# A half-swap of an 8192 x 8192 matrix by DMA: one issuing queue in place of two

## The chip, the cores and the metric

The kernel runs on one core of a Trainium2 chip. Its time is the time of one execution on the device, in microseconds (us), given as the median of several runs. One further execution was recorded by the hardware profiler; all durations inside the kernel come from that one.

The core has compute engines (TensorE, VectorE, ScalarE, GpSimd) that this kernel does not use, and 16 DMA engines, which copy bytes between memories. A DMA is asked for by an instruction on one of the sequencers, here SP (the sync queue, `nc.sync`) or ACT (the scalar queue, `nc.scalar`). The asking is called an issue; the copying is done later by the DMA engines, packet by packet. Input and output both lie in the chip's large memory, HBM.

## The reference

```
def setup_inputs():
    return {"x": np.random.randn(8192, 8192).astype(np.float32)}

def reference(x):
    return np.fft.ifftshift(x)
```

With even sizes, `ifftshift` moves the element at row r, column c to row (r + 4096) mod 8192, column (c + 4096) mod 8192. The four quarters of the matrix change places crosswise; nothing is computed. 8192 x 8192 x 4 bytes = 268.44 MB are read and as many are written.

## The kernel before

The whole kernel is a list of copies from HBM to HBM. There is no on-chip buffer and no compute instruction.

A row has `C` = 8192 elements, 32 KB; half a row, `hc` = 4096 elements, is 16 KB and lies in one piece. The loop at line 27 walks over the output in groups of 512 rows (`ENGINES * per` = 16 x 32), so it has 16 rounds. In a round, `src_row` (line 28) is the first row of the source group, 4096 rows further on, modulo 8192. The inner loop at line 29 makes two DMAs:

- on `nc.sync` with `h` = 0: it writes the left halves of the 512 output rows and reads the right halves of the 512 source rows (column offset `hc - h` = 4096);
- on `nc.scalar` with `h` = `hc`: it writes the right halves and reads the left halves.

Both use the access pattern `dims` of line 26, read from the outside in: 16 rows that follow one another (step `C`), for each of them 32 rows that are 16 rows apart (step `16 * C`), and for each of these 4096 elements in one piece. The outermost dimension has the size 16, as many as there are DMA engines; an engine's share is 32 half rows, row e, e + 16, e + 32 and so on. One DMA moves 512 x 16 KB = 8.39 MB, and there are 32 of them, 16 on each queue.

Nothing in the program depends on anything else, since every output element is written once and the input is never written. The order on each queue is the order of the loop. The framework gives the DMAs eight completion semaphores in turn; a DMA that is to use one again waits until the one that used it before has landed. With the two queues taking turns, that is the DMA four places earlier on the same queue. At the end SP waits for all that is still under way.

Of the kernel before, what the change touches and what calls it, by code (L numbers as in the profile page):

```python
# [1 line left out]

# [4 lines left out]


ENGINES = 16


@with_exitstack
def kernel(
    ctx: ExitStack,
    tc: tile.TileContext,
    x: bass.AP,
    out: bass.AP,
):
    nc = tc.nc
    R, C = x.shape  # L20
    hr = R // 2
    hc = C // 2


    per = 32
    dims = [[C, ENGINES], [ENGINES * C, per], [1, hc]]
    for row in range(0, R, ENGINES * per):
        src_row = (row + hr) % R
        for queue, h in ((nc.sync, 0), (nc.scalar, hc)):
            queue.dma_start(  # L30
                out=bass.AP(out.tensor, out.offset + row * C + h, dims),
                in_=bass.AP(x.tensor, x.offset + src_row * C + hc - h, dims),
            )


# [1 line left out]
_INS = ['x']  # L37
_OUTS = [((8192, 8192), 'float32')]


def kernel(**inputs):
    import numpy as _np
    import concourse.bacc as _bacc
    import concourse.tile as _tile
    from concourse import mybir as _mybir
    from concourse.bass_utils import run_bass_kernel_spmd as _run

    nc = _bacc.Bacc("TRN2", target_bir_lowering=False, num_devices=1)  # L48
    arrays, args = {}, []
    for name in _INS:  # L50
        a = _np.ascontiguousarray(inputs[name])
        if a.dtype.kind in "iu":
            a = a.astype(_np.int64)
        arrays[f"in_{name}_dram"] = a
        args.append(nc.dram_tensor(f"in_{name}_dram", a.shape, _mybir.dt.from_np(a.dtype), kind="ExternalInput").ap())
    for i, (shape, dtype) in enumerate(_OUTS):
        dt = _mybir.dt.from_np(_np.dtype(dtype))
        args.append(nc.dram_tensor(f"out_{i}_dram", shape, dt, kind="ExternalOutput").ap())
    with _tile.TileContext(nc) as tc:
        kernel(tc, *args)  # L60
    r = _run(nc, [arrays], core_ids=[0])
    got = tuple(r.results[0][f"out_{i}_dram"] for i in range(len(_OUTS)))
    return got[0]
```

## Time and profile before

| | us |
|---|---|
| median of 3 runs | 823.65 |
| lowest and highest | 820.24, 824.01 |
| the profiled execution | 822.98 |
| its span, from first to last instruction | 821.2 |

The profiled execution is the one that the page and all queries show. "Span" runs from its first to its last instruction.

In the page's second part the span is cut into 40 equal slices: the row `DMA` gives, in tenths, how busy the 16 DMA engines were on average, the row `GB/s` how much they moved (counted once, not for read and write separately). The third part has one row for each DMA queue: packets, megabytes, and the time that its packets took as a share of 16 engines over the whole span. A query can be given a window of the span, and then answers for that window alone. For DMA issues the profile also gives the duration of the issuing instruction and the time from its start until the data had landed:

| line 30 | issues | shortest issue, us | median issue, us | longest issue, us |
|---|---|---|---|---|
| on SP | 16 | 0.571 | 41.264 | 47.309 |
| on ACT | 16 | 0.579 | 42.036 | 48.448 |

From issue to landing the median is 204.0 us on SP and 204.1 us on ACT; over all issues the shortest is 51.6 and the longest 207.1 us. SP's issues begin at 0.7 us and the last begins at 614.2 us; ACT's last begins at 618.8 us. After that both sequencers only wait for transfers to finish.

### The profile page before, as it was taken

To read this page: it belongs to the slowest core of one execution; us is meant where nothing else is said; L and a number is where in the kernel's file an instruction comes from. 1 tells how busy PE (TensorE), PEld (TensorE's weight loads), DVE (VectorE), ACT (ScalarE), POOL (GpSimd) and SP (SyncE) were. 2 spreads that over 40 slices of the span, in tenths; PEclk is the share of its full clock that TensorE was granted. 3 is DMA by queue.
4 is the path that set the end of the run, shared out by engine and by line. 5 is a ranking of instruction groups with operands and counts; after the bars stand their busy time and mean duration, and the time that the engine had idled before them with its cause. 6 is when DMAs were issued, how large, how long until landed. Compare 5 with 4: busy or idle time off the path is not lost. (4 is left out here: it accounts for less than half of the span.)

```text
span 821.2 us, 77 instructions
## 1 busy us (share of the span) xinstructions
POOL 0.2 (0%) x4
## 2 busy tenths in 40 slices
POOL 0000000000000000000000000000000000000000
DMA  8999999999999999999999999999999999999998
GB/s 296 333 324 329 331 328 334 330 330 329 327 330 329 331 326 332 332 327 328 330 330 330 330 323 330 324 330 330 332 326 329 330 322 333 329 329 327 330 329 276
DMA packets 16896, 268.44 MB, mean 327 GB/s; under 512 B 512, under 2 KB 512, under 8 KB 512
## 3 DMA queue, kind: packets, MB, share of 16 engines
q1 hardware_dynamic: 8448, 134.22, 50.2%
q10 hardware_dynamic: 8448, 134.22, 49.0%
HBM read 268.44 MB, written 268.44 MB: 654 GB/s over the span
## 5 line engine op out<-in xcount | busy, mean ns | idle before, releaser
L48 POOL MEMSET const-bfloat16-1.0<- 128x1 bf16 x1 | 0.1, 102 | 0.0
L48 POOL MEMSET const-uint8-127<- 128x1 uint8 x1 | 0.1, 102 | 0.0
L48 POOL MEMSET const-float32-0.0<- 128x1 f32 x1 | 0.1, 99 | 0.2 <-issue 0.2
L48 POOL MEMSET const-float32-1.0<- 128x1 f32 x1 | 0.1, 99 | 0.0
## 6 DMA issues: line engine op xcount, KB each, us to landing
out_dram<-in_x_dram ACTq DMA_DIRECT2D x16, 8192.0 KB, 204.1
out_dram<-in_x_dram SPq DMA_DIRECT2D x16, 8192.0 KB, 204.0
```

Source lines behind the costliest of these rows:

```text
L48: nc = _bacc.Bacc("TRN2", target_bir_lowering=False, num_devices=1)
```

## The change

The inner loop no longer chooses a queue. Both DMAs of a round are issued on `nc.sync`, first the one that writes the left halves of the 512 rows, then the one that writes the right halves of the same rows.

```
--- before
+++ after
     for row in range(0, R, ENGINES * per):
         src_row = (row + hr) % R
-        for queue, h in ((nc.sync, 0), (nc.scalar, hc)):
-            queue.dma_start(
+        for h in (0, hc):
+            nc.sync.dma_start(
                 out=bass.AP(out.tensor, out.offset + row * C + h, dims),
                 in_=bass.AP(x.tensor, x.offset + src_row * C + hc - h, dims),
             )
```

The 32 DMAs, their sizes, their access patterns and their order in the program are the same. SP has 32 issues instead of 16, and ACT has none. The eight completion semaphores are still given in turn, so a DMA now waits for the one eight places earlier on the same queue.

## The prediction

> **What bounds the kernel now.** I read the page first. No compute engine does anything (POOL is busy for 0.2 us); the chain of waits is empty beyond the first half microsecond. What is left is the DMA part:
>
> ```profile
> span 821.2 us, 77 instructions
> ...
> DMA  8999999999999999999999999999999999999998
> GB/s 296 333 324 329 331 328 334 330 330 329 327 330 329 331 326 332 332 327 328 330 330 330 330 323 330 324 330 330 332 326 329 330 322 333 329 329 327 330 329 276
> DMA packets 16896, 268.44 MB, mean 327 GB/s; under 512 B 512, under 2 KB 512, under 8 KB 512
> ...
> q1 hardware_dynamic: 8448, 134.22, 50.2%
> q10 hardware_dynamic: 8448, 134.22, 49.0%
> HBM read 268.44 MB, written 268.44 MB: 654 GB/s over the span
> ```
>
> The two queues together keep 16 engines busy for 99.2% of the span, 0.992 x 821.2 = 814.6 us. Each engine moves 1024 of the 16,384 data packets (268.44 MB / 16,384 = 16 KB, half a row), so a packet takes 814.6 / 1024 = 0.795 us. (The 512 small packets, 16 for each of 32 DMAs, announce completions.) The other 0.8%, 6.6 us, is the head and the tail. So the time is 1024 x T + 6.6 us, T being the mean packet time, and the change must act on T or open gaps between packets.
>
> Is T = 0.795 us what an engine needs? The trace has two stretches in which one queue is alone. In the first microseconds only q1 has packets: the second table below is the window from 3.7 to 5.1 us. At the end q1 has finished its data and q10 is alone: the window from 815.4 to 817.5 us. (q1 is SP's: in the first 60 us SP's DMAs land after a median of 152.9 us, ACT's after 156.8, and q1 is ahead.)
>
> ```profile
> DMA packets 36, 0.59 MB, mean 421 GB/s; under 512 B 0, under 2 KB 0, under 8 KB 0
> ...
> q1 hardware_dynamic: 36, 0.59, 101.9%
> ```
>
> ```profile
> DMA packets 56, 0.67 MB, mean 320 GB/s; under 512 B 15, under 2 KB 15, under 8 KB 15
> ...
> q10 hardware_dynamic: 45, 0.66, 88.3%
> q1 hardware_dynamic: 11, 0.02, 4.0%
> ```
>
> In the first, 16 full engines move 421 GB/s, a packet in 16 x 16,384 B / 421 GB/s = 0.623 us. In the second, 0.66 MB take 0.883 x 16 x 2.1 = 29.7 engine-us: 22.2 GB/s per engine, 356 GB/s for 16, 0.736 us per packet. (Some engines have run dry, which is why the plain rate is 320.) The body, by the same sum, is at 16 x 16,384 / 0.795 = 330. So with one queue alone packets were quicker, at both ends. That is the strongest thing the trace says about this change, and it is thin: 1.4 and 2.1 us. Windows of 2.1 us in the middle, where both queues run, scatter as widely:
>
> ```profile
> 400.00:402.10 2.10, 0.00 (x0) 1.00 0.91 296
> 402.10:404.20 2.10, 0.00 (x0) 1.00 1.07 351
> ...
> 412.60:414.70 2.10, 0.00 (x0) 1.00 0.98 320
> 414.70:416.80 2.10, 0.00 (x0) 1.00 1.01 359
> ```
>
> (Columns: window, its length, POOL's busy time, clock, DMA share, GB/s.) The end stretch is at the top of that scatter; the start stretch is above it.
>
> **The change part by part.**
>
> 1. *ACT's 16 DMA issues go, SP gets 16 more.* Issuing is no path here if the queue never runs dry. The row of line 30 gives SP's issues 0.571 us at least and 41.3 us in the median: the long ones stand blocked until the queue has room. SP's fourth issue ended 46.4 us after the first began, when most of the first DMA's data had moved; so one queue takes in about three DMAs, 3 x 8.39 MB = 25 MB, 76 us of work at 330 GB/s. 32 issues at 0.571 us are 18 us in 821, all under transfers. Cost nothing; the cover is those 76 us, and it is lost only if SP is late by more than that. Behind a blocked issue on SP stand only the next issues and the final waits; nobody else waits for SP. ACT's queue is then empty, which costs nothing.
>
> 2. *The waits.* SP waited 123.8 us in 11 waits on earlier DMAs in the first 600 us, each for the DMA four places back on its own queue (51.3 us the longest), always with other DMAs queued. In one stream these waits fall on older DMAs. Bounds: no gain (the engines were full) and no loss (the same 76 us of cover). I take 0.
>
> 3. *The start.* The first packet moves 2.2 us into the span and is SP's; it stays. ACT's packets came in after 5.1 us (the window up to there holds none), when SP's had all engines busy (DMA share about 1.0 from 2.2 us on): 0. The end: 3.7 us after 817.5, the last engines and the landing. One queue ends with the same uneven engines: 0, at most -2 to +2 us.
>
> 4. *What lies side by side changes: the whole case.* Before, each engine alternates between the queues: a right half read to the left, then, from a row some steps behind, a left half to the right. In the first 20 us q1 has 208 packets and q10 154, so ACT trails by 54 / 16 = 3.4 packets per engine, and as engine e's rows are 16 apart, by some 54 rows or 1.8 MB. After, all 16 engines work in one such place at a time, and for 25 us the reads are all right halves and the writes all left ones. No row has this for long. Upper bound of the gain: T = 0.623, 1024 x 0.623 + 6.6 = 645 us. Next row: T = 0.736, 754 + 6.6 = 760 us. No gain: 821. Loss: see the last rival. The two quick stretches are short, and the longer is the less quick. I take half of what the end stretch shows, since it lies within the scatter of ordinary windows: T = (0.736 + 0.795) / 2 = 0.766, 784 + 7 = 791 us.
>
> A rule speaks against this. The Trainium skill, "DMA: Bandwidth & Descriptors", section "Issuing engines are not separate DMA queues", says that DMAs from different issuing engines interleave on the same 16 engines, so that several issuers save issue time and no more. The one-queue stretches at 421 and 356 GB/s beside 330 don't bear that out, weakly; by the rule the sum is 821 again. The same page, "Latency and other measured facts", reports copies whose rows lie 2 MiB apart at 164 GB/s where 512 KiB apart gave 207, and guesses at aliasing in HBM; ACT's trail of 1.8 MB is near that. Should that ratio (0.79) be the whole loss of the body, an estimate from that page is 0.79 x 815 + 7 = 651 us of span; no run here shows it.
>
> **Sum.** 791 us of span for the forecast. Around the profiled execution's 821.2 us lie 1.8 us (its time is 822.98), and the median of the runs shown is 823.65, 0.7 above it. 791 + 1.8 = 793 us, 3.7% under the median.
>
> **The rivals.**
>
> *No change, 823 us.* The engines and HBM carry the same bytes in packets of the same size; 654 GB/s of reads and writes is the limit of the path, and 421 at the start is what buffers take in before it fills. For it: 38 of the 40 slices lie at 322 to 334 GB/s whatever rows are moved. Against it: the windows by microsecond fall only as q10 comes in (377 and 455 GB/s up to 5.1 us, 393, 328 and 377 after it), and the end stretch is quick long after any start. A chance of 0.19.
>
> *The start rate lasts, 647 us.* If the two streams hinder each other in HBM and one doesn't, T stays near 0.623: 645 + 1.8. For it: 36 packets at that rate, from all 16 engines. Against it: the end stretch is not that quick, and reads and writes still meet. With what lies between it and the forecast's own range (under 750 us) 0.12.
>
> *Slower: one queue stumbles at the end of each DMA, 842 us.* Every DMA ends on every engine with a completion packet, after which the next DMA's packets begin. Before, the other queue's packets stand ready at that moment; after, nothing else does. Price: what the engines lost as they began. The first microsecond of packets moved 246 GB/s against 421 soon after, (421 - 246) / 421 = 0.42 us lost. At 31 boundaries 13 us; at 0.8 us, were the next one late as well, 25: 836 to 848, middle 842. If each DMA drained as the kernel's end does, 3.7 us, it would be 115 us more: 938. It decides from 4 / 31 = 0.13 us per boundary. Against it: queued DMAs lie 76 us deep, and the packets of successive DMAs on one queue stand one behind another. For it: no row of the trace shows such a boundary uncovered. The same outcome comes if 16 engines on the same half of neighbouring rows get in each other's way. 0.33.
>
> *That the change doesn't do what it says:* all 32 DMAs stand on SP in the changed program, 16 x 32 x 4096 elements each, none on ACT; excluded.
>
> **How the numbers follow.** The forecast, faster within 750 to 819 us, has 0.36; its own range is the two ends of T, 762 to 819. Something under about 0.5%, 4 us, can't be told from no change here (the three runs span 3.8 us). Faster: 0.36 + 0.12 = 0.48; same 0.19; slower 0.33. The range from 725 to 865 leaves out most of the start rate (some 0.09 of its 0.12) and of the slower case the drains (some 0.10).
>
> **What would show it.** In the profile after: one queue with 16,896 packets and 268.44 MB; its share, times the span, over 1024 gives T. T of 0.766 and a share of 99% or more confirm step 4; T of 0.795 the first rival. Body slices around 340 GB/s are the forecast, 328 no change, 415 the start rate. A share clearly below 99% means gaps: the slower rival, to be seen as dips about every 25 us. Issues should land after about 100 us in the median, four DMAs of 25 us, instead of 204. A body slower than 322 GB/s with a full queue would mean that step 4 has the wrong sign: the place side by side matters, but against one stream.

## The result, and the profile after

The changed kernel takes 824.64 us in the median of 20 runs (822.78 to 829.12), the kernel before 821.97 us in the median of as many on the same chips (819.22 to 827.0). The ratio is 1.0032, with a 95% interval of 1.0017 to 1.0047. By the bound of 0.5% this is no change; a cost of 0.2 to 0.5% is nevertheless clear of the noise. The forecast was 793 us; the time is that of the first rival (no change, 823 us). The ratios in this document are those of the record and not exactly quotients of two medians. One run of "halves by four" and one of "ACT far" below lay over 1.5% above the fastest of their kernel and are not in those ratios.

The profiled execution of the changed kernel took 826.81 us, 2.2 us more than its median, so its span should not be compared with the old one to the microsecond. Its page, the parts on the DMA engines:

```profile
span 825.0 us, 77 instructions
...
GB/s 289 321 330 322 319 333 323 307 327 329 331 326 321 329 324 325 330 320 338 326 333 328 330 328 329 326 333 325 327 328 330 334 326 330 330 329 328 328 330 292
...
q1 hardware_dynamic: 16896, 268.44, 99.3%
HBM read 268.44 MB, written 268.44 MB: 651 GB/s over the span
...
out_dram<-in_x_dram SPq DMA_DIRECT2D x32, 8192.0 KB, 108.2
```

There is one queue, and it keeps 16 engines busy for 99.3% of the span: 819.2 us, which over 1024 packets is 0.800 us each, against 0.795 before. The other 5.8 us are head and tail (6.6 before). (This execution was 2.2 us longer than the median one; without these 2.2 us T would be 0.798.) With 5.8 us in all in which the engines are not busy, there is no room for gaps at the ends of DMAs of the size that the slower rival priced, 13 us and more. The slices of the body lie at 307 to 338 GB/s, the lowest of them in the first 170 us. Nothing was gained, and next to nothing lost.

The view that decides the prediction's main argument is the first microseconds, window by window (columns: window, length, POOL, clock, DMA share, GB/s). First the kernel before, whose second queue comes in after 5.1 us, then the changed kernel:

```profile
3.20:4.20 1.00, 0.00 (x0) 1.00 0.93 377
4.20:5.10 0.90, 0.00 (x0) 1.00 1.10 455
5.10:6.10 1.00, 0.00 (x0) 1.00 1.03 393
6.10:7.10 1.00, 0.00 (x0) 1.00 1.02 328
7.10:8.10 1.00, 0.00 (x0) 1.00 1.08 377
8.10:9.10 1.00, 0.00 (x0) 1.00 0.97 311
```

```profile
2.20:3.20 1.00, 0.00 (x0) 1.00 0.98 229
3.20:4.20 1.00, 0.00 (x0) 1.00 1.09 410
4.20:5.10 0.90, 0.00 (x0) 1.00 0.94 400
5.10:6.10 1.00, 0.00 (x0) 1.00 1.07 377
6.10:7.10 1.00, 0.00 (x0) 1.00 1.10 344
7.10:8.10 1.00, 0.00 (x0) 1.00 0.86 311
8.10:9.10 1.00, 0.00 (x0) 1.00 1.19 410
9.10:11.10 2.00, 0.00 (x0) 1.00 0.93 311
11.10:13.10 2.00, 0.00 (x0) 1.00 1.05 311
```

A window of 1 us holds only some 20 to 25 packets, so single rows scatter (410 once more from 8.1 us on); taken together they are clear. From 3.2 to 5.1 us the changed kernel moved 405 GB/s on average (414 before), in the next 4 us 360 (352 before), and then it is down at the pace of the body. The start is as quick as before and slows at the same time. But here no second queue exists that could have come in. The quick start belongs to the start, not to having one queue alone.

The prediction's other quick stretch lay some 4 to 6 us before the end. Two neighbouring windows at about that place in the changed kernel, whose span is 825.0 us:

```profile
817.00:819.00 2.00, 0.00 (x0) 1.00 1.05 369
819.00:821.00 2.00, 0.00 (x0) 1.00 1.05 295
```

Under one queue the rate there is once well above the body's and once well below it, so the stretch shows scatter and no effect of the queue.

Two more views answer the steps on issues and waits, SP's row of line 30 and SP's waits over the whole span:

```profile
L30 SPq DMA_DIRECT2D out_dram<-in_x_dram x32: 612/24786/56487, 0.7 to 715.4; - x32
...
DMA to landing us min/median/max: 29.0/108.2/137.2
```

```profile
SPq L59 <- DMA out_dram<-in_x_dram: 84.3, 4, 25.5
```

SP stands in its issues (median 24.8 us, waiting for room in the queue) and waits for DMAs only in the closing part of the program, four times. No issue waits on the semaphore of an earlier DMA; before, SP had spent 123.8 us of its first 600 in such waits without any cost.

### The profile page after: what moved, and what is told of

The parts are those of the page before. It is cut to its first block, busy times and chain, and to the rows that moved or that the text cites. A ratio compares the mean times of both kernels' runs of the same rounds, so it can differ in the third digit from the quotient of the medians.

```text
span 825.0 us, 77 instructions
## 1 busy us (share of the span) xinstructions
POOL 0.2 (0%) x4
## 3 DMA queue, kind: packets, MB, share of 16 engines
q1 hardware_dynamic: 16896, 268.44, 99.3%
## 6 DMA issues: line engine op xcount, KB each, us to landing
out_dram<-in_x_dram SPq DMA_DIRECT2D x32, 8192.0 KB, 108.2
```

## The experiments

The kernel before was timed on the same chip beside each of the three groups. The three chips were a little quicker than those of the result: the medians of the kernel before are 813.4 to 813.9 us on them. So times are compared by ratio, and packet times of the experiments with 16 engines lie near 0.785 us.

**What sets the packet time?** Three theories were open: a path that all engines share (A), the engine's own pace (B), or one direction of the traffic (C, D). The first two runs take engines away. In the changed kernel's loop the outermost dimension, 16, becomes n:

```
+    for row, n, per in blocks:          # 384 rows: n = 12, per = 32; 512 rows: n = 8, per = 64
+        dims = [[C, n], [n * C, per], [1, hc]]
         for h in (0, hc):
             nc.sync.dma_start(
```

> One queue (SP) as in the changed kernel, same bytes in 16 KB packets, but 15 of every 16 rows are copied by 12 DMA engines instead of 16 (the last 256 rows of each half of the matrix by 16). Per engine 1280 packets in the 12-engine part and 64 in the rest. Theory A, all engines share one path to memory whose total of about 650 GB/s of reads and writes sets the packet time: 12 engines ask for less, packets get quicker, near the quickest packets seen (0.62 us at the start): 0.62 to 0.67 us, 1280 x 0.65 + 64 x 0.8 + 7 = about 890 us (850 to 915). Theory B, 0.795 us is what one engine needs for a copy once it is under way, whatever the others do: 1344 x 0.795 + 7 = 1076 us.

> One queue, all copies by 8 DMA engines, 2048 packets of 16 KB each. Theory A (shared path): no contention left, packets at the floor of 0.61 to 0.63 us, 2048 x 0.62 + 7 = 1277 us (1255 to 1300). Theory B (the engine's own pace): 2048 x 0.795 + 7 = 1635 us.

Measured: 12 engines 835.5 us, a ratio of 1.0279 (1.0228 to 1.0331); 8 engines 1249.56 us, 1.5373 (1.5298 to 1.5449). Two windows of 100 us of the body, first with 12 engines, then with 8:

```profile
100.00:200.00 100.00, 0.00 (x0) 1.00 0.75 322
200.00:300.00 100.00, 0.00 (x0) 1.00 0.75 324
```

```profile
100.00:200.00 100.00, 0.00 (x0) 1.00 0.50 216
200.00:300.00 100.00, 0.00 (x0) 1.00 0.50 216
```

The DMA share is over 16 engines, so 0.75 is 12 engines without a gap and 0.50 is 8. A packet takes 12 x 16,384 B / 322 GB/s = 0.611 us with 12 engines and 8 x 16,384 / 216 = 0.607 us with 8. Theory B is out: it asked for 1076 and 1635 us. Theory A holds, and both times lie even below its ranges (850 to 915 and 1255 to 1300), because the packets took less than the 0.62 to 0.67 and 0.61 to 0.63 us that these ranges were built on. At 12 engines the engines' own pace is the limit, at 16 the shared path. 12 engines move 322 GB/s; 16 move 328 on the chip of the first profile and some 333 on the quicker ones. The last four engines bring about 3%, and otherwise only longer packets for all.

The next two leave out one direction each. The reading kernel copies from HBM into eight on-chip tiles in turn, the writing kernel from one tile to all of the output:

```
+    dims = [[C, 128], [1, hc]]
+            t = pool.tile([128, hc], x.dtype)
+            nc.sync.dma_start(out=t[:], in_=bass.AP(x.tensor, x.offset + src_row * C + hc - h, dims))
...
+            nc.sync.dma_start(out=bass.AP(out.tensor, out.offset + row * C + h, dims), in_=t[:])
```

> Leaves out the writing to HBM (but for the last half tile): the same 268 MB are read in 16 KB packets, in the same order of halves per 128 rows, into on-chip buffers. Theory A, with reads and writes adding up on the shared path: half the memory traffic, packets at the engine's floor of 0.61 to 0.63 us, 1024 x 0.62 + 7 = 642 us (630 to 660). Theory C, reading alone is what limits: about 820 us. Theory B: 820 us.

> Leaves out the reading from HBM but for one tile: that on-chip tile is written over the whole output, 268 MB in 16 KB packets. Theory A: 0.61 to 0.63 us per packet, 642 us (630 to 660). Theory D, writing alone is what limits: about 820 us. Theory B: 820 us.

Measured: 639.0 us for reading (0.7862, 0.7823 to 0.79), 640.8 us for writing (0.7884, 0.7845 to 0.7922), both within theory A's 630 to 660 and far from the 820 of B, C and D. The page of the reading kernel, then a line of the writing kernel's:

```profile
GB/s 366 430 430 428 430 428 431 431 428 428 428 428 428 428 428 428 428 429 428 428 428 427 428 431 428 429 429 429 430 430 431 428 428 428 429 428 428 428 428 331
...
q1 hardware_dynamic: 18576, 270.54, 99.8%
HBM read 268.44 MB, written 2.10 MB: 424 GB/s over the span
```

```profile
HBM read 2.10 MB, written 268.44 MB: 423 GB/s over the span
```

With one direction alone, 16 engines on one queue run at 428 GB/s, 0.612 us per packet, for 600 us on end. So neither reading nor writing alone holds the copy at 328; both together do, at 328 + 328 = 656 GB/s of memory traffic. These two kernels have an on-chip end where the copy has HBM, so they show that the two directions together bind, not where on the way between them. They also show that a single queue can feed 16 engines at their full pace.

**Do queue, order of halves or distance matter?** Two more theories are for the 0.3%: H puts it down to all engines being on one half at a time, Q to having one queue. Four kernels change one of these each: two queues on the same half; the changed kernel with each DMA cut into 8; the same with the halves taking turns after every 4 packets; and the kernel before with ACT working on the other half of the rows.

```
 two queues, one half
+    for top in range(0, R, 512):
+        for h in (0, hc):
+            for queue, row in ((nc.sync, top), (nc.scalar, top + 256)):     # per = 16
 eight times the boundaries
+        for h in (0, hc):
+            for row in range(top, top + 512, 64):                          # per = 4, nc.sync
 halves by four
+    for row in range(0, R, 64):
+        for h in (0, hc):                                                  # per = 4, nc.sync
 ACT far
+            row = (top + h // hc * hr) % R                                 # two queues, per = 32
```

> Two queues again, but both work on the same half at a time: of 512 rows SP takes the first 256 and ACT the other 256, first all left halves, then all right halves; 64 DMAs of 4.2 MB. Theory A (only the traffic counts): ratio to before 1.000 (0.997 to 1.003). Theory H, the 0.3% of the change comes from all engines being on one half: 1.003 or more. Theory Q, the 0.3% comes from having one queue: 1.000. My step 4 of the prediction (one half at a time is quicker): 0.96.

> One queue, the packets of each engine in exactly the order of the changed kernel, but each DMA cut into 8, so 256 DMAs and 255 boundaries per engine in place of 31. The slower rival (a stumble at the end of each DMA): if the 2.7 us of the change are 31 boundaries, 0.087 us each, then 255 cost 22 us: ratio 1.027. Theory A: boundaries cost no more than their completion packet of 9 ns, 224 x 0.009 = 2 us more than the changed kernel: 1.003 to 1.007.

> One queue, 256 DMAs of 64 rows, left and right halves taking turns after every 4 packets of an engine, so that at most times engines on both halves lie side by side. To be held against the run with 8 times the boundaries, which differs in this order alone. Theory H (one half at a time costs 0.3%): quicker than that run by 0.003 or more. Theory A: the same within 0.003. My step 4: slower than that run by 0.03 or more.

> The kernel before with ACT's queue starting at the other half of the rows: ACT no longer trails SP by some 1.8 MB but works 134 MB away. The thought that the trail costs time (part of step 4): ratio clearly below 1, 0.96 or less. Theory A: 1.000 (0.997 to 1.003).

| run | queues | ratio to before | 95% interval |
|---|---|---|---|
| two queues, one half | 2 | 0.9997 | 0.9975 to 1.0018 |
| eight times the boundaries | 1 | 1.0029 | 1.0002 to 1.0055 |
| halves by four | 1 | 1.0020 | 0.9994 to 1.0046 |
| ACT far | 2 | 0.9984 | 0.9959 to 1.0009 |

The first and the third say that one half at a time is worth nothing: it gains nothing with two queues (0.96 was asked for by step 4), and mixing the halves in one queue loses nothing (0.03 was asked for). Nor does it cost the 0.3% of theory H, which asked for 1.003 or more in the first run, where the interval ends at 1.0018; the third differs from the second by only 0.0009, which is within the noise of both. The fourth says that ACT's trail of 1.8 MB cost nothing. The second rules out the slower rival: 255 boundaries in place of 31 should have cost 1.027 if the 0.3% lay there. Its interval ends at 1.0055, and 1.0029 is at the lower end of what theory A named (1.003 to 1.007).

**More on engines, queue and addresses.** If 12 engines move nearly all that 16 do, would 13 or 14 be better than 16? And does ACT's queue alone behave as SP's does, and do rows farther apart matter?

```
 fourteen, thirteen engines:  blocks of 448 or 416 rows, n = 14 or 13, per = 32, two queues as before
 ACT alone
-            nc.sync.dma_start(
+            nc.scalar.dma_start(
 rows together
-    dims = [[C, ENGINES], [ENGINES * C, per], [1, hc]]
+    dims = [[per * C, ENGINES], [C, per], [1, hc]]
```

> Two queues as before, but nearly all rows copied by 14 engines instead of 16 (the last 64 rows of each half of the matrix by 16). At the quickest packet of 0.611 us 14 engines would move 375 GB/s, more than the 328 of the body. Theory A, a shared path with a fixed total: it still binds, ratio to before 1.00 (0.995 to 1.01). Theory A', the path loses a little when 16 engines crowd it (12 engines had moved 322 GB/s with packets of 0.623 us, 16 move 328 with 0.795): fewer engines waste less, ratio 0.97 to 0.99.

> As the run with 14 engines, with 13 (the last 352 rows of each half of the matrix by 16): at most 348 GB/s at 0.611 us per packet. Theory A: 1.00 (0.995 to 1.015). Theory A': 0.96 to 0.99.

> The changed kernel with all 32 DMAs on ACT's queue instead of SP's: a second look at one queue against two, on the same chip as the others. If having one queue costs the 0.3%: ratio 1.002 to 1.005. If the 0.3% was something of SP's queue alone: 1.000.

> Two queues as before, but each engine's 32 rows of a DMA follow one another, so that the 16 engines work 1 MiB apart instead of 32 KB apart. Theory A in its plain form, only bytes count: 1.00 (0.997 to 1.005). If the path's total depends on which addresses are side by side, in a way that queues and halves did not touch: away from 1 by 0.02 or more, either way.

| run | median, us | ratio to before | 95% interval |
|---|---|---|---|
| 14 engines | 854.35 | 1.0505 | 1.0477 to 1.0533 |
| 13 engines | 834.93 | 1.0264 | 1.0237 to 1.0292 |
| ACT alone | 814.5 | 1.0020 | 1.0002 to 1.0039 |
| rows together | 813.25 | 0.9999 | 0.9978 to 1.0020 |

ACT's queue alone measures 1.0020, the lower end of what was named for one queue as the cause; 1.000, which was named for something in SP's queue, lies just outside the interval. By the two medians the ratio would be only 1.0008, so this is weak. Rows 1 MiB apart change nothing.

Both expectations for 13 and 14 engines failed, in a way that none of the theories had foreseen. The windows of the kernel with 14 engines show where:

```profile
100.00:200.00 100.00, 0.00 (x0) 1.00 0.87 333
200.00:300.00 100.00, 0.00 (x0) 1.00 0.88 332
300.00:400.00 100.00, 0.00 (x0) 1.00 0.89 333
770.00:800.00 30.00, 0.00 (x0) 1.00 0.51 217
800.00:830.00 30.00, 0.00 (x0) 1.00 0.50 215
```

(The expectation gives the packets of 12 engines 0.623 us; in the body they took 0.611, as above.) The body moves 333 GB/s with 14 engines up to 400 us, no less and no more than with 16 on this chip (the middle slices of the run with ACT alone are at 325 to 340); from 600 to 750 us it is 324 to 327. So the total of the path is nearly the same whether 14 or 16 crowd it, and theory A' is out: fewer engines waste nothing less. But from 770 us on the share is a half, which is 8 of 16 engines, and the rate 215 to 217 GB/s, which is what 8 engines move by themselves. The engines had equal shares of the rows, so they did not get equal shares of the path: six of the 14 had finished some 80 us before the span's end at 850.3, and the others went on without them. With 13 engines the same end is shorter (216 GB/s from 775 to 800 us, and 215 to 820). Which engines they are, and why, was not looked into. With 16 engines it does not show: there the end is ragged by a few microseconds only. No kernel here that does the whole copy beats the kernel before by more than its interval.

## Why the prediction was wrong

- *The reading of the bound* held: 1024 x T plus a fixed head and tail. It is 1024 x 0.800 + 5.8 after.
- *Step 1, the issues at no cost,* held. 32 issues on one sequencer are covered by the queue, and the landing took 108.2 us in the median, where about 100 had been named.
- *Step 2, the waits at 0,* held; they vanished and nothing changed, because the engines had been full anyway.
- *Step 3, head and tail at 0,* held: 5.8 us against 6.6.
- *Step 4 failed.* It took "half of what the end stretch shows", T = 0.766 us, as the gain from one queue being alone. T came out at 0.800: the engines were not held up by a second queue, but by a limit on reads and writes together, at 651 GB/s after and 654 before. Of its two pieces of evidence, the start at 421 GB/s is a start-up: the changed kernel has the same start and the same fall from 5 us on without a second queue, and the 428 GB/s that lasted 600 us with one direction left out shows what is missing later, room for reads and writes together. The end stretch at 356 GB/s lay within the scatter of ordinary windows (up to 359 in the middle), as the prediction itself noted; half of a scatter's top was taken for an effect. The end of the changed kernel, with 369 and 295 GB/s side by side under one queue, shows it to be scatter. The step's mechanism, that all engines on one half at a time are quicker, was tried by itself too: 0.9997 with two queues, and the halves mixed in one queue cost nothing (1.0020 against 1.0029).
- *The first rival* was described rightly, a limit of the path for reads and writes together, and was given only 0.19. The argument that kept it low, that the rate fell "only as q10 comes in", was a coincidence in time, since the rate falls as much where no q10 exists. What spoke for it, 38 of 40 slices within 322 to 334 GB/s whatever rows were moved, was the better evidence: nearly the whole span against 3.5 us.
- *The start rate lasting* is out for a copy; it does last when one direction is left out. *The stumble at DMA ends* is out by the run with 255 boundaries, and its other form, that engines on the same half get in each other's way, by the run with two queues on one half (0.9997).
- *The two rules* that the prediction cites from the Trainium skill, page "DMA: Bandwidth & Descriptors", sections "Issuing engines are not separate DMA queues" and "Latency and other measured facts". That several issuers save issue time and no more fits all seven kernels with 16 engines and HBM on both sides of the copy, to about 0.3%. The slowing of copies whose rows lie 2 MiB apart was not tested, as no run here has that pitch. What the prediction drew from it, a loss through ACT's trail of 1.8 MB, did not appear: moving ACT 134 MB away gave 0.9984.

What stays open is the 0.2 to 0.3%. The four kernels with one queue measure 1.0032, 1.0029, 1.0020 and 1.0020, the three others with two queues 0.9997, 0.9984 and 0.9999. So it seems to go with the number of queues, not with SP, the order of halves or the boundaries. One of the four intervals reaches below 1. What in one queue costs these 2 us was not found: in single profiles it is smaller than the spread between executions. The profiles hint at where it is lost. From 20 to 60 us the four kernels with one queue moved 320, 325, 323 and 322 GB/s, and the four with two (the kernel before, then the three others) 329, 330, 333 and 335. From 400 to 780 us there is no such difference (329 in the changed kernel and 328 before; 334 against 333 in the others). Some 3% of 40 us is an estimate of 1.2 us, about half of what is missing. That is one profile of each kernel, and no run tested why.

## What to carry to other kernels

When a copy keeps every DMA engine busy, find out first whether the engines or something that they share is the limit: take a quarter of the engines away. If the time hardly moves (here 2.8%), something shared is the limit, and a change that leaves the bytes alone needs a reason of its own to help; here no order of queues, halves or rows did. Do not take a rate from the first microseconds of a kernel (here 405 to 414 GB/s against 328 later), nor from one short window whose like can be found in the body. A change of the number of engines must also be watched at its end, where unequal shares show.

## What was not expected of the hardware

Twelve DMA engines copy HBM to HBM at 322 GB/s with 0.611 us per 16 KB packet, sixteen at 328 with 0.795 to 0.800: the path holds about 330 GB/s of copying, 656 GB/s of reads and writes, however many engines from 13 to 16 share it. From 3.2 to 5.1 us, at the start, it gave 405 to 414. And engines with equal work do not always finish together: with 14 of them the body ran at 333 GB/s, and then a part of them went on alone at 216 GB/s for some 80 us.
